# Attention in a two-layer decoder trunk: scores and values as products on halves of the array, denominators ahead of the transposes, two orders changed

## The chip, the cores and the metric

The kernel runs on one core of one Trainium2 chip. The metric is the device time of one execution in microseconds (us); lower is better. The engines are PE (TensorE matmul; PEld is its weight load), DVE (VectorE), ACT (ScalarE), POOL (GpSimd) and SP, which here only issues transfers.

## The reference, cut to what matters

The trunk has 256 positions, a width of 1024 and two layers. Each layer is a feed-forward block (width 2816), a mixer, and another feed-forward block. The mixer of the first layer joins a sliding-window attention with a multi-scale pooling; the mixer of the second is a recurrence (RWKV7). The attention, which the change is about:

```python
q = rms_norm(q, q_norm)          # 8 heads of 64
k = rms_norm(k, k_norm)          # 2 heads of 64, each serves 4 query heads
scores = einsum('bnqhgd,bnkhd->bhgnqk', qb, kb) * 64 ** -0.5
scores = where(valid, scores - slopes * dist, -inf)      # window of 128 positions
m = maximum(max(scores), sink)
p = exp(scores - m)
denom = sum(p) + exp(sink - m)
out = einsum('bhgnqk,bnkhd->bnqhgd', p / denom, vb)
```

The queries of positions 0 to 127 see one block of 128 keys; those of positions 128 to 255 see two blocks, so 256 keys.

## The kernel before, in words

The 256 positions are two halves `h` = 0 and 1 of 128 rows each. Projections and feed-forward products are made of three products on high and low parts of the numbers in fp32r (`mm3`, L225 to L227). The weights are loaded in pieces of 128x1024 (`split`), cast by ACT to the high part (`whi`, L215); DVE or POOL make the low part (`wlo`, L220, L218). The small products of attention, pooling and recurrence are in f32; each of them stands in the trace as two instructions on PE (transposes as one).

**Layer 0's mixer** is cut into steps, and the string `ORDER_AB` (L34) says in which order they are written. `I` projects keys, values, queries and the pooling input of a half (`ab_in`). `N1` normalizes the rows of the second half. `P` is the pooling (`ab_pool`, L440): ACT scales the accumulator into `p` (L442), four band products (L448, in the second half also L450), ACT's copy of the means `mp` (L452), four products with `pool_w` (L455), DVE's scale (L456) and `hilo` (a cast on ACT, L288, and a subtraction on DVE, L289), which writes one half of the columns for the output projection. `K`, `Q`, `S`, `E`, `F` are the five parts of `ab_mix` (L459), each up to a `yield`:

- `K`: the keys are normalized (power and scale on POOL), written twice side by side into `kd`, transposed, and copied by ACT into `kbd` (L481), a block-diagonal tile that was zeroed once (L403): rows 0 to 63 hold the keys for one query head, rows 64 to 127 the same keys for the other.
- `Q`: the queries are normalized in the same way and transposed; `qT` holds two heads in its 128 rows.
- `S`: for each pair of heads one product on all 128 rows gives the scores of both side by side (L506, 2 x 128 columns in the first half, 2 x 256 in the second). DVE adds the distance term for each head (L509) and takes the maximum of each pair (L512).
- `E`: maximum with the sink, then eight exponentials on ACT, one for each head, with the sum in the accumulator (L523); the denominators and their reciprocals `rden` on DVE (L525, L527).
- `F`: PE transposes the exponentials (L536), ACT and DVE copy them to `pT` (L538, L540). With `pT` as the loaded operand (128 columns) and 64 columns of values moving, PE makes `ops` (L545). DVE multiplies by `rden` (L547), PE transposes the result (L550), and `hilo` makes the attention half of the input of the output projection.

`O` is that projection (`ab_out`, with `w_out`), which takes the pooling's columns first (`ABP`); `B` begins the feed-forward block behind it (norm, transposes on PE, eight casts with the gain on ACT, L299). The PSUM banks of a half are taken in turn from two names: `ms` and `gu`, or `tp` and `gu`, where `gu` has two buffers.

**Layer 1's mixer** is written in the order of the string `ORDER` (L32). Two of its steps matter. `k00` is `c_gram` for the first eight heads and the first rows: two grams on 64x64 halves (`heads2`, L733), each followed by a masking on DVE (L816), transposes (`turn2`, L740) and a copy on ACT (L819). `d00` is `c_rest`: products (L893), a masking on DVE (L895) and three rounds of products and an addition on DVE (L904). Both take their banks in turn from the same four, `acc00` to `acc11`. Near them stands `t1` (`c_substitute`), a chain of small DVE instructions (L853, L855) that begins with what a transfer through DRAM brings (`L<-ds`).

The order in which instructions are written is not the order in which they run: the framework's scheduler simulates the engines and gives each engine a fixed list, by priority (the written order) among what its simulation takes to be ready. On the chip each engine goes through its list in order.

Of the kernel before, what the change touches and what calls it, by code (L numbers as in the profile page):

```python
# [8 lines left out]
F32 = mybir.dt.float32  # L9
F32R = mybir.dt.float32r  # L10
BF16 = mybir.dt.bfloat16
AF = mybir.ActivationFunctionType
ALU = mybir.AluOpType
AX = mybir.AxisListType
# [14 lines left out]
QB = (0, 0)  # L29
QV = (0, 0)  # L30
NPT = 2
ORDER = 'L k o0 r p00 R p01 b00 b01 s0 o1 p10 p11 v g V t0 D0 X l0 b11 b10 s1 D1 d00 k00 k01 k11 t1 d01 k10 v10 v01 l1 d10 c00 c10 d11 v00 c01 v11 W0 P00 P01 O00 c11 P10 P11 O10 Y W1 O01 a0 O11 a1'  # L32
BIG = 8
ORDER_AB = 'I0 N1 K0 Q0 S0 P0 E0 I1 K1 Q1 P1 F0 S1 E1 F1 O0 B0 O1 B1'  # L34
ABP = (2, 3, 0, 1)
POOL_AB = 2
ABB = (('ms', 'gu'), ('tp', 'gu'))
# [1 line left out]
HALVES = (slice(0, 64), slice(64, 128))  # L39
# [87 lines left out]
def bc(ap, axis, n):  # L127
    a = ap.unsqueeze(axis)
    shape = list(a.shape)
    shape[axis] = n  # L130
    return a.broadcast_to(shape)


class Trunk:
# [263 lines left out]
    def ab_setup(self):  # L398
        nc, A = self.nc, self.A
        s = self.ab = {}  # L400
        self.mixer_pool("ab")
        s["kbd"] = self.mx.tile([128, 2, 2, 256], F32, name="kbd")
        nc.gpsimd.memset(s["kbd"], 0.0)  # L403
        def load(n, shape, src=None):
            a = self.now.rearrange("p a (b c) -> p a b c", b=2) if len(shape) == 4 else self.now
            return self.const(n, shape, src=src, pool=self.mx, after=a[:, 0] if len(shape) == 2 else a)

        s["qkg"] = load("qk_gain", [128, 2])
        s["sink"] = load("sink", [128, 8], A["sinks"][0].partition_broadcast(128))
        s["ps"] = load("pool_scale", [128, 4])  # L410
        s["edge"] = load("edge", [128, 4, 16])
        s["dist"] = load("dist", [128, 256])
        s["pw"] = load("pool_w", [128, 4, 128])
        s["band"] = load("band", [128, 4, 2, 128])
        s["v"] = [self.mx.tile([128, 2, 64], F32, name=f"v{h}") for h in range(2)]
        s["p"] = [self.mx.tile([128, 512], F32, name=f"p{h}") for h in range(2)]
# [42 lines left out]
    def ab_mix(self, h, st):  # L459

        nc, A, ab = self.nc, self.A, self.ab
        acc, kv, r0, bank = st["acc"], st["kv"], st["r"], st["bank"]
        one, small = self.mx, self.msmall
        v, kbd = ab["v"][h], ab["kbd"]

        tk = small.tile([128, 128], F32, name=f"tk{h}", bufs=1)
        nc.scalar.activation(out=tk, in_=kv[:, :128], func=AF.Square, scale=r0)
# [6 lines left out]
                                in1=bc(bc(rk, 2, 2), 3, 64), op=ALU.mult)  # L474
        nc.scalar.activation(out=v, in_=kv[:, 128:].rearrange("p (a b) -> p a b", a=2), func=AF.Copy, scale=r0)
        kps = bank([128, 2, 128])
        for a in range(2):
            nc.tensor.transpose(kps[:, a, :], kd[:, a].rearrange("p a b -> p (a b)"), self.ident)
        for b in range(2):
            r = slice(64 * b, 64 * b + 64)  # L480
            nc.scalar.activation(out=kbd[r, :, b, 128 * h:128 * h + 128], in_=kps[r], func=AF.Copy,  # L481
                                 scale=ab["qkg"][r, 1:2])
        yield

        tq = one.tile([128, 512], F32, name=f"tq{h}")
# [6 lines left out]
                                in0=acc[0].rearrange("p (a b) -> p a b", a=8), in1=bc(rq, 2, 64), op=ALU.mult)  # L492
# [3 lines left out]
        qT = one.tile([128, 4, 128], F32, name=f"qT{h}")  # L496
# [3 lines left out]
        k0 = 0 if h else 128  # L500
        nk = 256 - k0
        s = one.tile([128, 8, nk], F32, name=f"s{h}")
        mx = small.tile([128, 8], F32, name=f"mx{h}")
        for i in range(4):
            sps = bank([128, 2, nk])
            nc.tensor.matmul(sps, qT[:, i, :], kbd[:, i // 2, :, 0:nk], start=True, stop=True)  # L506
            for j in range(2):

                nc.vector.scalar_tensor_tensor(out=s[:, 2 * i + j, :], in0=ab["dist"][:, k0:],  # L509
                                               scalar=-8.0 * 2.0 ** -(2 * i + j + 1), in1=sps[:, j, :],  # L510
                                               op0=ALU.mult, op1=ALU.add)
            nc.vector.tensor_reduce(out=mx[:, 2 * i:2 * i + 2], in_=s[:, 2 * i:2 * i + 2, :], axis=AX.X, op=ALU.max)  # L512
        yield

        nc.vector.scalar_tensor_tensor(out=mx, in0=mx, scalar=0.125, in1=ab["sink"], op0=ALU.mult, op1=ALU.max)
# [9 lines left out]
        nc.vector.tensor_tensor(out=den, in0=den, in1=es, op=ALU.add)  # L525
        rden = small.tile([128, 8], F32, name=f"rden{h}")
        nc.vector.reciprocal(out=rden, in_=den)  # L527
        yield
        nb = nk // 128
        mh, ml = st["x"]  # L530
        pT = one.tile([128, nb, 8, 128], F32, name=f"pT{h}")
        for b in range(nb):
            for q in range(2):
                tp = bank([128, 4, 128])
# [3 lines left out]
                    nc.scalar.copy(out=pT[:, b, 4 * q:4 * q + 4, :], in_=tp)  # L538
                else:
                    nc.vector.tensor_copy(out=pT[:, b, 4 * q:4 * q + 4, :], in_=tp)  # L540
        ops = bank([128, 8, 64])
        for i in range(8):
            for b in range(nb):
                vv = ab["v"][h - nb + 1 + b]
                nc.tensor.matmul(ops[:, i, :], pT[:, b, i, :], vv[:, i // 4, :], start=b == 0, stop=b == nb - 1)  # L545
        o = one.tile([128, 512], F32, name=f"tq{h}")
        nc.vector.tensor_tensor(out=o.rearrange("p (a b) -> p a b", a=8), in0=ops, in1=bc(rden, 2, 64), op=ALU.mult)  # L547
        tp = bank([128, 4, 128])
        for i in range(4):
            nc.tensor.transpose(tp[:, i, :], o[:, i * 128:(i + 1) * 128], self.ident)  # L550
        self.hilo(tp, mh.tiles[0], ml.tiles[0])
        yield

# [505 lines left out]
def trunk(tc, A, out, stop=None):  # L1059
    with ExitStack() as ctx:  # L1060
# [49 lines left out]
        for h in range(2):  # L1110
# [4 lines left out]
            for n in "KQSEF":  # L1115
                do[f"{n}{h}"] = lambda h=h: next(mix[h])
        for n in ORDER_AB.split():
            do[n]()
        with t.pool("pre") as t.pre:
# [20 lines left out]
            def tail(h):  # L1140
                t.add_acc(h, t.cs["acc", h])
                t.ffn_begin(S[3], h, 3)
# [13 lines left out]
            for G in range(2):  # L1156
# [16 lines left out]
                do[f"a{G}"] = lambda h=G: tail(h)  # L1173
            for n in ORDER.split():
                do[n]()
# [24 lines left out]
```

## Time and profile before

| what | us |
|---|---|
| median of three runs (lowest, highest) | 1110.58 (1107.48, 1113.06) |
| the profiled execution's own time | 1113.11 |
| its span, first to last instruction | 1111.3 |
| PE busy in the span | 1056.5 |
| DVE busy | 640.1 |
| ACT busy | 517.1 |
| POOL busy | 206.5 |

The profile is that of one execution. Busy times are sums over the whole span, while the change touches two short stretches of it: layer 0's mixer, from about 206 to 291 us, and a part of layer 1's mixer, near 800 us. So the rows below are cut by stretch. In the rows of the timeline the first number is the start in us, the second the time from there to the end of the last instruction of the row; several instructions of one kind in a row are merged, with their count as x2, x16. An idle time stands in brackets, with what ended it. Instructions of PE overlap: the time that one costs is the distance of the starts, and not its duration.

### The profile page before, as it was taken

To read this page: it belongs to the slowest core of one execution; us is meant where nothing else is said; L and a number is where in the kernel's file an instruction comes from. 1 tells how busy PE (TensorE), PEld (TensorE's weight loads), DVE (VectorE), ACT (ScalarE), POOL (GpSimd) and SP (SyncE) were. 2 spreads that over 40 slices of the span, in tenths; PEclk is the share of its full clock that TensorE was granted. 3 is DMA by queue.
4 is the path that set the end of the run, shared out by engine and by line. 5 is a ranking of instruction groups with operands and counts; after the bars stand their busy time and mean duration, and the time that the engine had idled before them with its cause. 6 is when DMAs were issued, how large, how long until landed. Compare 5 with 4: busy or idle time off the path is not lost.

```text
span 1111.3 us, 16514 instructions
## 1 busy us (share of the span) xinstructions
PE 1056.5 (95%) x6332; PEld 856.9 (77%) x6332; DVE 640.1 (58%) x966; ACT 517.1 (47%) x876; POOL 206.5 (19%) x199
## 2 busy tenths in 40 slices
PE   7999999999999999999999999998698889999998
PEld 5788887778788888778888877875697667888886
DVE  6655454566564554665555546897574666464642
ACT  7544444574554443554444435675122355454440
POOL 2101110340300101010101101174201530101100
PEclk9999999999999999999999999999899798999999
DMA  8764664453465555556565544652422246555631
GB/s 288 245 208 160 228 193 139 149 175 101 141 220 188 194 164 191 170 156 196 165 222 158 183 121 127 181 161 53 110 61 67 69 144 218 207 186 174 204 99 38
DMA packets 70671, 179.33 MB, mean 161 GB/s; under 512 B 23872, under 2 KB 24512, under 8 KB 70592
## 3 DMA queue, kind: packets, MB, share of 16 engines
q1 hardware_dynamic: 70304, 178.19, 50.5%
q8 instruction: 50, 0.82, 0.3%
q14 instruction: 29, 0.24, 0.1%
q10 hardware_dynamic: 288, 0.09, 0.0%
HBM read 174.58 MB, written 3.67 MB: 160 GB/s over the span
## 4 chain that ended last, share of the span: by engine, by line
PE 81%; DVE 6%; DMA 4%; ACT 4%; issue 3%; POOL 1%; SPq 0%; DVEq 0%; ACTq 0%; POOLq 0%
PE gu L225 14%; PE gu L227 14%; PE gu L226 14%; PE acc L225 10%; PE acc L227 10%; PE acc L226 10%; DMA raw<-w_gu 2%; DVE wlo L220 2%; PE acc L733 2%; PE tp L351 2%; ACT whi L215 1%; PE gu L733 1%; DMA hn<-w_rkvo 1%; PE tp L733 1%; PE ms L733 0%
## 5 line engine op out<-in xcount | busy, mean ns | idle before, releaser
L220 DVE TENSOR_TENSOR wlo<-raw,whi 128x1024 fp32r<-128x1024 f32 x261 | 341.0, 1308 | 182.5 <-ACT whi L215 179.2
L215 ACT CAST whi<-raw 128x1024 fp32r<-128x1024 f32 x306 | 320.6, 1049 | 198.1 <-PE gu L227 72.8
L225 PE MATMUL gu<-whi,xh 128*128 128x512 f32 x704 | 286.7, 408 | 2.5 <-ACT xh L299 2.2
L227 PE MATMUL gu<-whi,xl 128*128 128x512 f32 x704 | 279.2, 398 | 2.0 <-DVE xl L300 1.8
L226 PE MATMUL gu<-wlo,xh 128*128 128x512 f32 x704 | 279.4, 397 | 0.1
L218 POOL TENSOR_TENSOR wlo<-raw,whi 128x1024 fp32r<-128x1024 f32 x45 | 108.3, 2407 | 616.3 <-ACT whi L215 610.8
L227 PEld LDWEIGHTS gu<-whi,xl 128*128 128x128 f32 x704 | 133.4, 189 | 35.6 <-DVE xl L300 4.8
L225 PEld LDWEIGHTS gu<-whi,xh 128*128 128x128 f32 x704 | 133.4, 190 | 33.1 <-ACT xh L299 6.2
L226 PEld LDWEIGHTS gu<-wlo,xh 128*128 128x128 f32 x704 | 133.7, 190 | 27.5 <-DVE wlo L220 0.6
L225 PE MATMUL acc<-whi,ah 128*128 128x512 f32 x352 | 139.0, 395 | 4.0 <-ACT ah L288 4.0
L226 PE MATMUL acc<-wlo,ah 128*128 128x512 f32 x352 | 137.5, 391 | 0.0
L227 PE MATMUL acc<-whi,al 128*128 128x512 f32 x352 | 131.1, 394 | 0.1
L342 ACT ACTIVATE t<-gu,rh 128x256 f32<-128x256 f32 x88 | 41.4, 473 | 119.9 <-PE gu L227 119.9
L343 DVE SCALAR_TENSOR_TENSOR t<-t,gu 128x256 f32<-128x256 f32 x88 | 36.6, 418 | 87.3 <-ACT t L342 87.2
L289 DVE TENSOR_TENSOR al<-tp,ah 128x256 fp32r<-128x256 f32 x88 | 37.1, 421 | 84.5 <-ACT ah L288 84.4
L288 ACT CAST ah<-tp 128x256 fp32r<-128x256 f32 x88 | 32.4, 369 | 111.0 <-PE tp L351 110.9
L225 PEld LDWEIGHTS acc<-whi,ah 128*128 128x128 f32 x352 | 66.0, 188 | 20.4 <-ACT ah L288 5.7
L227 PEld LDWEIGHTS acc<-whi,al 128*128 128x128 f32 x352 | 65.8, 188 | 15.6 <-DVE al L289 0.5
L226 PEld LDWEIGHTS acc<-wlo,ah 128*128 128x128 f32 x352 | 66.1, 188 | 15.0
L226 PE MATMUL acc<-wlo,xh 128*128 128x512 f32 x160 | 64.5, 403 | 0.0
L227 PE MATMUL acc<-whi,xl 128*128 128x512 f32 x160 | 63.9, 405 | 0.6 <-DVE xl L289 0.6
L225 PE MATMUL acc<-whi,xh 128*128 128x512 f32 x160 | 62.4, 408 | 0.7 <-ACT xh L288 0.7
(495 smaller groups left out, 1117.6 us busy)
## 6 DMA issues: line engine op xcount, KB each, us to landing
raw<-w_gu SPq DMA_DIRECT2D x176, 512.0 KB, 4.3
raw<-w_dn SPq DMA_DIRECT2D x88, 512.0 KB, 4.2
raw<-w_rkvo SPq DMA_DIRECT2D x24, 512.0 KB, 3.6
raw<-w_qp SPq DMA_DIRECT2D x8, 512.0 KB, 4.3
raw<-w_out SPq DMA_DIRECT2D x8, 512.0 KB, 3.5
hn<-w_rkvo SPq DMA_DIRECT2D x16, 256.0 KB, 2.8
ch<-chan SPq DMA_DIRECT2D x10, 256.0 KB, 5.1
x<-x SPq DMA_DIRECT2D x4, 256.0 KB, 5.2
```

The lines of the kernel that those rows point to most:

```text
L215: nc.scalar.copy(out=hi, in_=raw)
L218: nc.gpsimd.tensor_tensor(out=lo, in0=raw, in1=hi.bitcast(F32), op=ALU.subtract)
L220: nc.vector.tensor_tensor(out=lo, in0=raw, in1=hi.bitcast(F32), op=ALU.subtract)
L225: mm(out, xh, wh, start=start, stop=False)
L226: mm(out, xh, wl, start=False, stop=False)
L227: mm(out, xl, wh, start=False, stop=stop)
L288: self.nc.scalar.copy(out=hi, in_=src)
L289: self.nc.vector.tensor_tensor(out=lo, in0=src, in1=hi.bitcast(F32), op=ALU.subtract)
L342: nc.scalar.activation(out=t, in_=gu[:, :256], func=AF.Tanh, scale=rh)
L343: nc.vector.scalar_tensor_tensor(out=t, in0=t, scalar=1.0, in1=gu[:, :256], op0=ALU.add, op1=ALU.mult)
L351: nc.tensor.transpose(ps[:, j, :], t[:, j * 128:(j + 1) * 128], self.ident)
L733: self.nc.tensor.matmul(out[rs], a[rs], b[rs], start=start, stop=stop)
```

## The change

- `kbd` and its memset go. `kT` (128 x 2 x 256) holds the transposed keys without zeros: rows 0 to 63 and rows 64 to 127 hold the same keys, and one ACT copy for each half of the positions writes it in place of two.
- Scores: for each group `a` of four heads two banks are taken, one for each half of the rows. Each product takes 64 rows of `qT` and of `kT` and gives the scores of one head; the two halves of the rows write to different banks. One maximum for four heads takes the place of one for two.
- Denominators: at the end of `E`, eight ACT instructions for each half of the positions scale the exponentials by `rden`, ahead of the transposes of `F`.
- Values: 64 columns of values are now the loaded operand and 128 columns of `pT` move. The two heads of a pair write to the two halves of the PSUM partitions, so the result comes out transposed; the multiplication by `rden` and the transposes of the output (L547, L550) go.
- Order: in `ORDER_AB` `P0` moves from behind `S0` to ahead of `Q0`, and `P1` from behind `Q1` to behind `E1`. In `ORDER` `k00` and `d00` change places.

```diff
-ORDER = '... s1 D1 d00 k00 k01 k11 t1 ...'
+ORDER = '... s1 D1 k00 d00 k01 k11 t1 ...'
-ORDER_AB = 'I0 N1 K0 Q0 S0 P0 E0 I1 K1 Q1 P1 F0 S1 E1 F1 O0 B0 O1 B1'
+ORDER_AB = 'I0 N1 K0 P0 Q0 S0 E0 I1 K1 Q1 F0 S1 E1 P1 F1 O0 B0 O1 B1'
...
-        s["kbd"] = self.mx.tile([128, 2, 2, 256], F32, name="kbd")
-        nc.gpsimd.memset(s["kbd"], 0.0)
+        s["kT"] = self.mx.tile([128, 2, 256], F32, name="kT")
...
-        for b in range(2):
-            r = slice(64 * b, 64 * b + 64)
-            nc.scalar.activation(out=kbd[r, :, b, 128 * h:128 * h + 128], in_=kps[r], func=AF.Copy,
-                                 scale=ab["qkg"][r, 1:2])
+        nc.scalar.activation(out=kT[:, :, 128 * h:128 * h + 128], in_=kps, func=AF.Copy, scale=ab["qkg"][:, 1:2])
...
-        for i in range(4):
-            sps = bank([128, 2, nk])
-            nc.tensor.matmul(sps, qT[:, i, :], kbd[:, i // 2, :, 0:nk], start=True, stop=True)
-            for j in range(2):
-                nc.vector.scalar_tensor_tensor(out=s[:, 2 * i + j, :], in0=ab["dist"][:, k0:],
-                                               scalar=-8.0 * 2.0 ** -(2 * i + j + 1), in1=sps[:, j, :],
-                                               op0=ALU.mult, op1=ALU.add)
-            nc.vector.tensor_reduce(out=mx[:, 2 * i:2 * i + 2], in_=s[:, 2 * i:2 * i + 2, :], axis=AX.X, op=ALU.max)
+        for a in range(2):
+            sps = [bank([128, 2, nk]) for b in range(2)]
+            for i in range(2):
+                for b, rs in enumerate(HALVES):
+                    nc.tensor.matmul(sps[b][:, i, :], qT[rs, 2 * a + i, :], kT[rs, a, 0:nk], start=True, stop=True)
+            for n in range(4):
+                j = 4 * a + n
+                nc.vector.scalar_tensor_tensor(out=s[:, j, :], in0=ab["dist"][:, k0:], scalar=-8.0 * 2.0 ** -(j + 1),
+                                               in1=sps[n % 2][:, n // 2, :], op0=ALU.mult, op1=ALU.add)
+            e = slice(4 * a, 4 * a + 4)
+            nc.vector.tensor_reduce(out=mx[:, e], in_=s[:, e, :], axis=AX.X, op=ALU.max)
...
+        for i in range(8):
+            nc.scalar.activation(out=s[:, i, :], in_=s[:, i, :], func=AF.Copy, scale=rden[:, i:i + 1])
         yield
...
-        ops = bank([128, 8, 64])
-        for i in range(8):
-            for b in range(nb):
-                vv = ab["v"][h - nb + 1 + b]
-                nc.tensor.matmul(ops[:, i, :], pT[:, b, i, :], vv[:, i // 4, :], start=b == 0, stop=b == nb - 1)
-        o = one.tile([128, 512], F32, name=f"tq{h}")
-        nc.vector.tensor_tensor(out=o.rearrange("p (a b) -> p a b", a=8), in0=ops, in1=bc(rden, 2, 64), op=ALU.mult)
         tp = bank([128, 4, 128])
         for i in range(4):
-            nc.tensor.transpose(tp[:, i, :], o[:, i * 128:(i + 1) * 128], self.ident)
+            for b in range(nb):
+                for j, rs in enumerate(HALVES):
+                    nc.tensor.matmul(tp[rs, i, :], ab["v"][h - nb + 1 + b][:, i // 2, :], pT[:, b, 2 * i + j, :],
+                                     start=b == 0, stop=b == nb - 1)
         self.hilo(tp, mh.tiles[0], ml.tiles[0])
```

## Rows read from the trace of the kernel before

**Rows 1.** The page, part 1: busy time, share of the span, instructions.

```profile
PE 1056.5 (95%) x6332; PEld 856.9 (77%) x6332; DVE 640.1 (58%) x966; ACT 517.1 (47%) x876; POOL 206.5 (19%) x199
```

**Rows 2.** Busy time by stretch (us, engines, granted clock, DMA share, GB/s).

```profile
206.00:291.00 85.00, 81.15 (x436) 66.70 (x435) 49.14 (x91) 47.15 (x107) 26.95 (x39) 1.00 0.40 125
...
796.00:805.00 9.00, 0.66 (x12) 0.42 (x10) 2.73 (x14) 0.00 (x0) 0.00 (x0) 0.80 0.57 126
291.00:745.00 454.00, 447.79 (x2034) 362.17 (x2033) 269.21 (x373) 222.33 (x349) 74.85 (x58) 1.00 0.55 176
```

**Rows 3.** Waits of PE from 206 to 291: total us, times, longest.

```profile
PE ms L455 <- ACT mp L452: 1.7, 1, 1.7
...
PE acc L227 <- DVE xl L289: 0.6, 1, 0.6
```

**Rows 4.** The chain that ended last, 200 to 300 us: start, us, what.

```profile
219.69 0.47 ACT kbd L481
...
221.88 0.43 PE ms L506 x2
...
255.10 0.86 PE tp L506 x2
...
256.89 0.44 PE ms L550 x4
```

**Rows 5.** Timeline of PE near 252 us: value products, then scores.

```profile
251.81 1.45 PE L545 MATMUL gu<-v,pT 128*128 128x64 f32 x12
253.10 1.08 PE L506 MATMUL gu<-kbd,qT 128*128 128x512 f32 x2
```

**Rows 6.** Timeline of PE from 745 us: full products, then 64x64 halves.

```profile
744.95 0.40 PE L227 MATMUL acc<-whi,xl 128*128 128x512 f32 x1
745.27 1.09 PE L733 MATMUL tp<-a,b 64*64 64x128 f32 x16
746.20 0.63 PE L740 MATMUL gu<-ident,b 64*64 64x64 f32 x16
746.66 1.04 PE L733 MATMUL gu<-a,b 64*64 64x128 f32 x16
747.54 0.63 PE L740 MATMUL ms<-ident,b 64*64 64x64 f32 x16
```

**Rows 7.** Timeline at 205 us: matmuls on the full array and a load.

```profile
205.17 0.39 PE L225 MATMUL acc<-whi,ah 128*128 128x512 f32 x1
205.17 0.19 PEld L226 LDWEIGHTS acc<-wlo,ah 128*128 128x128 f32 x1
...
205.40 0.40 PE L226 MATMUL acc<-wlo,ah 128*128 128x512 f32 x1
```

**Rows 8.** Timeline of ACT, 266 to 274 us: exponentials and gain casts.

```profile
266.64 0.49 ACT L523 ACTIVATE s<-s,nm 128x256 f32<-128x256 f32 x1
267.05 0.19 ACT L523 ACTIVATION_READ_ACCUMULATOR s<-s,nm 128x1 f32 x1
...
271.65 0.35 ACT L299 ACTIVATE xh<-acc,gain 128x128 fp32r<-128x128 f32 x1
...
273.30 0.62 ACT L299 ACTIVATE xh<-acc,gain 128x128 fp32r<-128x128 f32 x2
```

**Rows 9.** Timeline, 270 to 282 us: denominators, ACT's next idle time.

```profile
270.22 0.17 DVE L525 TENSOR_TENSOR den<-den,es 128x8 f32<-128x8 f32 x1 [1.16 <-ACT s L523]
...
281.57 0.47 ACT L342 ACTIVATE t<-gu,rh 128x256 f32<-128x256 f32 x1 [5.85 <-PE gu L227]
```

**Rows 10.** Timeline of layer 1's mixer, 801 to 811 us.

```profile
801.89 0.16 DVE L853 TENSOR_TENSOR pr<-L,XL 128x2 f32<-128x2 f32 x1 [7.49 <-DMA L<-ds]
...
804.76 2.26 PE L733 MATMUL acc<-tmp 64*64 64x64 f32 x32 [8.34 <-DVE tmp L904]
...
806.80 1.71 PE L733 MATMUL acc<-a,k 64*64 64x128 f32 x16
...
810.21 1.09 PE L733 MATMUL acc<-a,k 64*64 64x128 f32 x16 [1.23 <-DVE b L904]
```

More of the change, by code (lines that the diff above doesn't have):

```diff
@@ L31 @@
 NPT = 2
-ORDER = 'L k o0 r p00 R p01 b00 b01 s0 o1 p10 p11 v g V t0 D0 X l0 b11 b10 s1 D1 d00 k00 k01 k11 t1 d01 k10 v10 v01 l1 d10 c00 c10 d11 v00 c01 v11 W0 P00 P01 O00 c11 P10 P11 O10 Y W1 O01 a0 O11 a1'
+ORDER = 'L k o0 r p00 R p01 b00 b01 s0 o1 p10 p11 v g V t0 D0 X l0 b11 b10 s1 D1 k00 d00 k01 k11 t1 d01 k10 v10 v01 l1 d10 c00 c10 d11 v00 c01 v11 W0 P00 P01 O00 c11 P10 P11 O10 Y W1 O01 a0 O11 a1'
 BIG = 8
-ORDER_AB = 'I0 N1 K0 Q0 S0 P0 E0 I1 K1 Q1 P1 F0 S1 E1 F1 O0 B0 O1 B1'
+ORDER_AB = 'I0 N1 K0 P0 Q0 S0 E0 I1 K1 Q1 F0 S1 E1 P1 F1 O0 B0 O1 B1'
 ABP = (2, 3, 0, 1)
@@ L463, in ab_mix @@
         one, small = self.mx, self.msmall
-        v, kbd = ab["v"][h], ab["kbd"]
+        v, kT = ab["v"][h], ab["kT"]
         tk = small.tile([128, 128], F32, name=f"tk{h}", bufs=1)
```

## The prediction

> **What bounds the kernel now.** I read the page's first part, then the busy time by stretch, then who waited for whom on PE. PE is busy for 95% of the span [rows 1]. Nearly everything edited lies in the attention stretch from 206 to 291 us: there PE is busy for 81.15 of 85 us, at the full granted clock, while ACT has 47.15 us of work and DVE 49.14 [rows 2]. PE's waits there are few; the ones that count below are 1.7 and 0.6 us long [rows 3]. So this stretch is a stream of matmuls with short holes, and what is taken off PE's queue should show, as long as other matmuls are ready. The feed-forward stretch behind it (291 to 745 us) has PE busy for 447.79 of 454 us [rows 2], so time won earlier is carried through it. The swap of `k00` and `d00` lies in a different place: a hole of 9 us in layer 1 in which PE has 0.66 us of work and the clock's mean falls to 0.80 [rows 2].
>
> **Scores (L506).** Each f32 product is issued as two instructions. Two of them take 0.43 us with 256 columns (first half of the rows, four products) and 0.86 us with 512 (second half, four) [rows 4]: 1.72 + 3.44 = 5.16 us. The new form has twice as many products, each on 64 rows and with half the columns. If the two row halves of the array run side by side, the time is that of half the columns: 2.58 us, a gain of 2.58. No row shows 64 rows by 128 columns; the nearest is the gram of layer 1 on 64x64 halves, where 16 instructions of 128 columns take 0.88 us, 0.055 each [rows 6], half of the 0.107 that such an instruction needs alone by the scores' row (0.43/2 for 256 columns). The bounds are 0 and 2.58; I take 2.58, since the row shows halves side by side.
>
> **Values and probabilities (L545, L547, L550).** 48 instructions of 64 columns stand there; twelve take 1.29 us (251.81 to 253.10), 0.107 each [rows 5], so they cost 5.14 us and are set by the load of 128 columns rather than by the 64 that move. Eight transposes of the output at 0.44 us for four [rows 4] add 0.88. The new form also has 48 instructions, now of 128 moving columns on 64 loaded ones: 0.107 each if one after the other (nothing gained but the transposes), 0.055 side by side [rows 6], 2.57 us in all. Gain 0.88 to 3.45; I take 3.45 for the same reason. A multiplication on DVE per half goes too, at no gain: DVE is far from full.
> Here a row and a rule meet. The load for L226 starts at 205.17 us together with L225's matmul on all 128 rows, which is in flight until 205.56 [rows 7]. The Trainium skill, "TensorE: Matmul & The Clock Gate", Part 3, says that a weight load overlaps a matmul in flight only when it goes to another row group. By that rule the column halves, which all use every row, would load between matmuls: the values' gain would stay at its lower bound and the whole would come out at 1106.8 us. Rows 7, where the load runs under a matmul on the same rows, speak against it.
>
> **Changes of shape.** From a full-array matmul to one on halves takes 0.32 us (744.95 to 745.27) against 0.23 between two full ones (205.17 to 205.40): 0.09 [rows 6, 7]. I take the same on the way back. The scheduler mixes these groups with the output projection; two blocks for each of scores and values in each half make 8 blocks, 8 x 0.18 = 1.4 us of loss (bounds 0.7 with four blocks, 4.3 with every one of the 24 pairs alone).
>
> **Denominators on ACT.** Sixteen scalings are added. With 128 columns one gain cast of the next norm lasts 0.35 us and two last 0.62, so each follows the one before by 0.27; with 256 columns an exponential gives way to its accumulator's read after 0.41 us (266.64 to 267.05) [rows 8]. That is 8 x 0.27 + 8 x 0.41 = 5.4 us. Of the four copies into `kbd`, at 0.47 us, two go: -0.94 [rows 4]. Net +4.5 us on ACT. What covers them: ACT's work in the stretch is 47 of 85 us, and after its work of the second half it stood idle for 5.85 us [rows 2, 9]. But now the transposes of the probabilities wait for the denominators (270.22 us in the second half) and the scalings, where before they followed the exponentials, and behind the scalings in ACT's queue stand the gain casts of the next norm, which the first gate products need [rows 8, 9]. With no cover the cost is 5.4 us; with full cover 0. The scheduler can put projections and pooling there; I charge 1.5 us, about half of the second half's 3.3; the first half's scalings lie where the projection of the second half's rows keeps PE going.
>
> **Order of the stretch.** `P0` now comes ahead of `Q0`, `S0` and `E0`: three ACT passes of 512 columns (some 0.7 us each, an estimate from the 0.27 and 0.41 above), two DVE passes and 16 PE instructions of 128 columns (1.7 us at 0.107). It issues no DMA, nothing on SP and nothing on POOL; what it is moved past (`Q0`'s power and scale on POOL, its transposes, `E0`'s exponentials) it can hold up by those 2.1 us of ACT at most, and the projection `I1` keeps PE going then. Today it runs so late that PE waits 1.7 us for the copy of its means, and 0.6 us more for its low half before the output projection [rows 3]. Early pooling removes both: -2.3 us (bounds 0 and -2.3). `P1` goes behind `E1` and `F0` ahead of `S1`: the work of `P1` becomes filling for the second half's softmax, counted in the 1.5 above. The memset of `kbd` on POOL goes at no gain: no wait in the stretch is for it [rows 3].
>
> **`k00` ahead of `d00`.** DVE waits 7.49 us for the transfer of `L` at the head of `t1`; the update of `d00` behind it in DVE's queue holds PE for 8.34 us, and `k00`, which takes the same four banks later, can only run at 806.80 and 810.21 [rows 10]. Put first, it can run ahead of the hole: a gram with its transposes takes 1.34 us at full clock (746.20 to 747.54), its two 2.7 [rows 6]. Against it: `d00` starts later, so that more of its rounds fall behind the same DVE wait. One round costs PE 2.04 us at the lower clock (804.76 to 806.80). No DMA is issued by either. Bounds -2.7 and +2.0; I take -1.0: one of the two grams won, less a handover, since 806.80 shows half of `k00` standing between the hole and the next step.
>
> **Sum.** -2.58 - 3.45 + 1.4 + 1.5 - 2.3 - 1.0 = -6.4 us. The profiled execution took 1113.11 us, 1.8 of it around its span of 1111.3; so it would take 1106.7. It stands 2.5 above the median of the runs, so in terms of the median 1110.58 the forecast is 1104.2 us.
>
> **Rivals.**
> 1. *The halves don't overlap.* Then only the output's transposes are saved: -0.88 + 1.4 + 1.5 - 2.3 - 1.0 = -1.3, 1109.3 us. The 64x64 rows speak against it, but no row has 64 by 128 or 128 by 64, so 0.10. If it holds for the values alone, the loss is 2.57: 1106.8 us. The rule named above would lead to that half of it.
> 2. *ACT becomes the bound* (slower). In the softmax of each half PE finds nothing ready while ACT scales; then PE's savings only lengthen its waits, and the net ACT time counts: +4.5 - 1.0 = +3.5, 1114.1 us, and to 1116 and more if the casts of the next norm are late as well. It decides when the ready work in PE's queue is shorter than the 3.3 us of the second half's scalings. For it: the norm casts stand behind them. Against: ACT's 5.85 us of idleness right after, and the output projection as filling [rows 9]. 0.10.
> 3. *`d00` falls wholly behind the transfer.* Two more rounds at 2.04 us and a handover of 0.3 each (my guess), some 4.7 us, less the 2.7 of `k00`: +2.0 where I took -1.0, so 1107.2 us. 0.14.
> 4. *The time is given back.* The weights of the next feed-forward arrive at their own pace, so that the savings of the stretch turn into waits for casts: only the -1.0 is left, 1109.6 us. Against it: PE at 447.79 of 454 us and no long wait in the stretch for a cast of weights [rows 2, 3]. 0.06.
>
> **How the numbers follow.** My forecast has 0.60. Its own range is 1100 to 1108: from -2.7 in layer 1 and four blocks of shape changes to no gain in layer 1 and a charge of 3 on ACT. Half a per cent is 5.55 us, about what a measurement of this kernel can tell from no change; it is reached at 1105.0. About seven tenths of my forecast and some of rivals 3 and 1 lie beyond: faster 0.50. The rest of it and most of rivals 1, 3 and 4, with part of 2, make same 0.40; slower 0.10 is rival 2 with a bad layer 1. The range runs from 1099 to 1112, taking in rivals 1, 3 and 4 and leaving out rival 2 and the best ends.
>
> **What will show it.** Right: scores of 64 rows in pairs at about 0.11 (128 columns) and 0.21 us (256); the value products at about 0.055 each; no L550; no wait of PE for the copy of `P0`'s means; PE's stretch from 206 to its first steady gate product shorter by 5 us; `k00` before the 8 us hole. Wrong: pairs at double these times (rival 1), new waits of PE on the scalings or on the norm's casts of 3 us and more (rival 2), a longer hole and later `d01` in layer 1 (rival 3), PE waits on casts of weights after 291 us (rival 4).

## The result, and the profile after

The changed kernel takes 1125.66 us (median of 6 runs, 1121.4 to 1128.99) where the kernel before took 1112.07 beside it (6 runs): a ratio of 1.0123, 95% interval 1.0092 to 1.0153. It is slower, by 13.6 us; the forecast was 1104.2, and the range ended at 1112. The profiled execution took 1124.33 us, its span is 1122.5 us (before: 1113.11 and 1111.3).

The page's first part, busy time of each engine over the span [rows 1]:

```profile
PE 1065.6 (95%) x6340; PEld 861.9 (77%) x6340; DVE 640.1 (57%) x960; ACT 522.9 (47%) x890; POOL 208.3 (19%) x198
```

PE is 9 us busier than before, though its matmuls were to become cheaper. ACT has 5.8 us more where the prediction's net was 4.5: the sixteen scalings took 2.45 + 3.31 = 5.76, and the saving of two copies doesn't show in the sum.

To place the loss, I cut the program at the additions into the residual on DVE, which every version has. The attention of layer 0 lies between the last L372 ahead of it and the last L378 behind it. Timeline of DVE, kernel before:

```profile
207.80 0.69 DVE L372 SCALAR_TENSOR_TENSOR x<-acc,x 128x512 f32<-128x512 f32 x1
...
289.56 0.68 DVE L378 TENSOR_TENSOR x<-acc,x 128x512 f32<-128x512 f32 x1
```

And the same of the changed kernel:

```profile
207.52 0.69 DVE L372 SCALAR_TENSOR_TENSOR x<-acc,x 128x512 f32<-128x512 f32 x1
...
301.12 0.68 DVE L378 TENSOR_TENSOR x<-acc,x 128x512 f32<-128x512 f32 x1
```

The attention went from 289.56 - 207.80 = 81.8 us to 93.6: 11.8 us longer, against 11.2 us between the two profiled executions. The two feed-forward stages behind it take the same as before within 0.1 us, the mixer of layer 1 takes 1.0 us more (239.4 against 238.3) and the rest 1.6 less (0.3 ahead of the attention, 1.3 behind the mixer). So the time was lost in the attention, and nothing behind it gave it back. This cut is steady: two programs with the same attention, the kernel before and one that differs from it only in layer 1, gave 81.8 and 82.1; the changed kernel and such a sister of it 93.6 and 94.3.

Busy time by stretch of the changed kernel, columns as in [rows 2]:

```profile
206.00:291.00 85.00, 77.87 (x389) 60.35 (x388) 41.50 (x78) 46.43 (x111) 22.10 (x27) 0.88 0.28 91
253.00:273.25 20.25, 17.51 (x62) 12.45 (x62) 7.14 (x17) 11.70 (x46) 0.00 (x0) 0.50 0.00 1
260.00:270.00 10.00, 10.00 (x37) 7.28 (x36) 4.95 (x10) 2.63 (x10) 0.00 (x0) 0.50 0.01 2
```

Before, this stretch ran at a granted clock of 1.00 throughout. Now there are 20 us at 0.50, that is 1.2 of 2.4 GHz: PE is busy for 17.51 us there. At the full clock that would be work of about half the time (products of 512 columns start 0.43 us apart there, 0.23 at 1.00), so by estimate up to 8.8 us are lost to the clock; less, where other engines would have made PE wait. Waits of PE from 206 to 302 us [rows 3]:

```profile
PE gu L538 <- ACT s L529: 2.7, 1, 2.7
PE acc L227 <- DVE xl L289: 1.6, 1, 1.6
PE tp L491 <- DVE tq L487: 1.4, 1, 1.4
PE tp L505 <- DVE s L509: 0.9, 1, 0.9
PE tp L225 <- ACT xh L299: 0.3, 1, 0.3
PE gu L454 <- ACT mp L451: 0.2, 1, 0.2
```

Of the two waits that early pooling was to remove, the one for the copy of P0's means went from 1.7 to 0.2 us, as forecast; the one for its low half (L227 for L289) grew from 0.6 to 1.6. A new one stands at the head: the transposes of the probabilities (L538) wait 2.7 us for the scalings (L529). Where it comes from is seen in the timeline of all engines, cut to the steps that follow on one another:

```profile
217.52 0.69 DVE L487 TENSOR_TENSOR tq<-acc,rq 128x512 f32<-128x512 f32 x1 [2.50 <-POOL rq L486]
...
230.27 0.69 ACT L441 ACTIVATE p<-acc,rs 128x512 f32<-128x512 f32 x1 [2.26 <-PE acc L227]
...
235.75 0.72 PE L447 MATMUL ms<-band,p 128*128 128x128 f32 x5
...
237.15 1.16 PE L454 MATMUL gu<-mp,pool_w 128*128 128x128 f32 x8 [0.21 <-ACT mp L451]
238.14 0.60 PE L491 MATMUL ms<-ident,tq 128*128 128x128 f32 x4
...
240.71 0.37 PE L505 MATMUL gu<-kT,qT 64*128 64x128 f32 x1
240.72 0.37 PE L505 MATMUL ms<-kT,qT 64*128 64x128 f32 x1
...
252.51 1.59 PE L505 MATMUL tp<-kT,qT 64*128 64x256 f32 x4 [0.92 <-DVE s L509]
...
256.39 2.45 ACT L529 ACTIVATE s<-s,rden 128x128 f32<-128x128 f32 x8 [0.53 <-DVE rden L527]
...
256.84 1.35 PE L538 MATMUL gu<-ident,s 128*128 128x128 f32 x4 [2.74 <-ACT s L529]
```

The queries of the first half (`tq`) are ready at 218.2 us, but their transposes (L491) run at 238.14. Before, they ran at 218.97, by the timeline of PE:

```profile
218.97 0.60 PE L495 MATMUL ms<-ident,tq 128*128 128x128 f32 x4
```

Between the two stands P0. K0, P0 and Q0 of a half take their PSUM banks from one turn (`ABB`, `ms` and `gu` for the first half), in the order of the program. With P0 ahead of Q0, P0's band products hold `ms`, and Q0's transposes have to wait until they were made and copied out. P0 in turn needs the second column of the input projection, which ends at 230. So the part that could have started waits for the part that couldn't, and scores, exponentials and scalings of the first half come some 20 us later, next to those of the second half.

Where they ran in pairs, the products did what was forecast: for the first four heads of the first half, the two row halves start 0.01 us apart (240.71, 240.72); the other scores ran one row half after the other. Value products follow one another at 0.067 us (twelve in the 0.81 us from 281.29 to 282.10, the step back to full matmuls included):

```profile
281.29 0.88 PE L548 MATMUL gu<-pT,v 128*64 128x128 f32 x12
282.10 0.50 PE L225 MATMUL gu<-whi,xh 128*128 128x512 f32 x1
```

In layer 1 the grams and transposes of `k00` did run ahead of the hole, as forecast, but the hole stayed, with one round of `d00` behind it as before. Timeline of the changed kernel, the lines that answer to [rows 10]:

```profile
811.42 1.92 SPq L837 DMA_DIRECT2D L<-ds  x4
...
814.86 0.16 DVE L852 TENSOR_TENSOR pr<-L,XL 128x2 f32<-128x2 f32 x1 [8.17 <-DMA L<-ds]
...
817.17 1.12 PE L732 MATMUL acc<-tmp 64*64 64x64 f32 x16 [8.58 <-DVE tmp L903]
```

### The profile page after: what moved, and what is told of

It is laid out like the page before. It is cut to its first block, busy times and chain, and to the rows that moved or that the text cites. A ratio compares the mean times of both kernels' runs of the same rounds, so it can differ in the third digit from the quotient of the medians.

```text
span 1122.5 us, 16523 instructions
## 1 busy us (share of the span) xinstructions
PE 1065.6 (95%) x6340; PEld 861.9 (77%) x6340; DVE 640.1 (57%) x960; ACT 522.9 (47%) x890; POOL 208.3 (19%) x198
## 4 chain that ended last, share of the span: by engine, by line
PE 80%; DVE 6%; DMA 5%; ACT 4%; issue 3%; POOL 1%; SPq 1%; DVEq 0%; ACTq 0%; POOLq 0%
PE gu L225 14%; PE gu L227 14%; PE gu L226 14%; PE acc L225 10%; PE acc L227 10%; PE acc L226 10%; DVE wlo L220 2%; DMA raw<-w_gu 2%; PE tp L351 2%; ACT whi L215 1%; DMA hn<-w_rkvo 1%; PE gu L732 1%; PE acc L732 1%; PE tp L732 1%; PE ms L732 0%
## 5 line engine op out<-in xcount | busy, mean ns | idle before, releaser
L227 PE MATMUL gu<-whi,xl 128*128 128x512 f32 x704 | 278.5, 397 | 0.6 <-DVE xl L300 0.5
L227 PEld LDWEIGHTS gu<-whi,xl 128*128 128x128 f32 x704 | 133.2, 189 | 32.6 <-DVE xl L300 1.8
L227 PE MATMUL acc<-whi,al 128*128 128x512 f32 x352 | 131.0, 394 | 0.1
L289 DVE TENSOR_TENSOR al<-tp,ah 128x256 fp32r<-128x256 f32 x88 | 37.0, 421 | 82.8 <-ACT ah L288 82.8
L227 PEld LDWEIGHTS acc<-whi,al 128*128 128x128 f32 x352 | 65.8, 188 | 15.6 <-DVE al L289 0.5
L227 PE MATMUL acc<-whi,xl 128*128 128x512 f32 x160 | 63.9, 404 | 1.6 <-DVE xl L289 1.6
```

Of the source, the lines that this page charges most:

```text
L227: mm(out, xl, wh, start=False, stop=stop)
L289: self.nc.vector.tensor_tensor(out=lo, in0=src, in1=hi.bitcast(F32), op=ALU.subtract)
```

## The experiments

All of them in one table: median time, ratio to the kernel before run beside it with its interval, the length of the attention (last L372 to last L378, from the profile) and of layer 1's mixer (from the third of the four L372 that end the second feed-forward behind the attention, to the last L378). The two lengths are those of one profiled execution each.

| kernel | us | ratio | attention | layer 1 |
|---|---|---|---|---|
| before | 1112.07 | 1 | 81.8 | 238.3 |
| changed | 1125.66 | 1.0123 [1.0092, 1.0153] | 93.6 | 239.4 |
| e1 | 1122.37 | 1.0096 [1.0069, 1.0123] | 89.8 | 240.3 |
| e2 | 1116.01 | 1.0045 [1.003, 1.006] | 86.1 | 238.6 |
| e3 | 1107.56 | 0.9962 [0.995, 0.9974] | 76.6 | 238.5 |
| e4 | 1120.43 | 1.0081 [1.0062, 1.01] | 94.3 | 234.1 |
| e5 | 1105.98 | 0.9954 [0.9937, 0.9971] | 76.6 | 237.5 |
| e6 | 1112.09 | 0.9999 [0.9983, 1.0015] | 80.2 | 239.4 |
| e7 | 1116.51 | 1.0069 [1.0044, 1.0094] | 80.5 | 241.9 |
| e8 | 1112.77 | 1.0014 [1.0001, 1.0027] | 82.1 | 239.1 |
| e9 | 1114.99 | 1.0035 [1.0021, 1.0049] | 81.5 | 242.5 |
| e10 | 1106.26 | 0.995 [0.9931, 0.9969] | 77.1 | 238.4 |
| e11 | 1110.86 | 0.9993 [0.9978, 1.0007] | 79.2 | 239.0 |
| e12 | 1105.11 | 0.9947 [0.9926, 0.9967] | 76.6 | 237.7 |
| e13 | 1122.51 | 1.0102 [1.0076, 1.0128] | 90.7 | 239.5 |
| e14 | 1116.52 | 1.0053 [1.0037, 1.007] | 88.5 | 236.6 |

The kernel before had medians of 1110.7 to 1112.1 in the several comparisons.

**e1: the changed kernel with the attention's parts in the order of before.**

```
-ORDER_AB = 'I0 N1 K0 P0 Q0 S0 E0 I1 K1 Q1 F0 S1 E1 P1 F1 O0 B0 O1 B1'
+ORDER_AB = 'I0 N1 K0 Q0 S0 P0 E0 I1 K1 Q1 P1 F0 S1 E1 F1 O0 B0 O1 B1'
```

> The changed kernel with the old ORDER_AB alone. Bank theory (P0 written ahead of Q0 takes the bank ms first, Q0's transposes wait for it until 238 us, and the first half's softmax falls behind the projections): Q0's transposes back at about 218 us, the exponentials of the first half near 226 us, no stretch at half clock, 1104 to 1109 us, a little faster than before. ACT theory (the sixteen scalings, 5.8 us in the profile, set the pace): 1118 us or more, since they stay. Shape theory (products on halves let the clock fall): the half clock stays near 260 us, 1118 us or more.

Measured: 1122.37 us, attention 89.8. Q0's transposes are back at 219.07 us, as the bank theory had it, but its time is missed. The turn of the banks is therefore not the whole story: with P0 back, 8.0 us of loss against the kernel before remain in the attention. Waits of PE from 206 to 302 us:

```profile
PE gu L538 <- ACT s L529: 4.8, 1, 4.8
PE ms L454 <- ACT mp L451: 2.7, 1, 2.7
PE gu L225 <- ACT xh L299: 1.2, 1, 1.2
```

The scalings now hold PE for 4.8 us in the second half. What stands in ACT's queue there, by the timeline:

```profile
274.71 1.98 ACT L215 CAST whi<-raw 128x1024 fp32r<-128x1024 f32 x2
276.59 3.31 ACT L529 ACTIVATE s<-s,rden 128x256 f32<-128x256 f32 x8
279.79 0.60 ACT L299 ACTIVATE xh<-acc,gain 128x128 fp32r<-128x128 f32 x2
```

Casts of weights ahead of the scalings, the scalings, and the next norm's casts behind them: this is the mechanism of rival 2, with P1 no longer there to fill the time. The clock is at 0.50 twice here, for 3.4 us from 241.3 and for 6.8 us from 275.4; each time it falls during one of the first two waits.

**e2: the kernel before with the new order of the parts.** The reverse of that edit, on the kernel before.

> The kernel before with the new ORDER_AB alone: no products on halves, no scalings. Bank theory: Q0's transposes at about 238 us, the half clock appears here too, 1124 to 1132 us (more than the changed kernel, since the products are longer). ACT theory and shape theory: 1109 to 1114 us, as before.

Measured: 1116.01 us, attention 86.1, in the range of no theory. Q0's transposes run at 238.93 us, as the bank theory had it; the half clock that it expected didn't come: from 200 to 300 us the clock stays at 1.00. The order alone costs 4.3 us of attention there.

**e3: the changed kernel, the pool's products in banks of their own.** In `ab_pool` alone `bank` becomes a turn over the two banks of the half's accumulator, which are free once the projections were read (cut out of a longer assignment).

```
-bank = st["bank"]
+bank = self.banks((f"acc{h}0", f"acc{h}1"))
```

> The changed kernel, its order kept, but the pooling takes its two banks from the accumulators that it has just read (acc01, acc00 in the first half, acc11, acc10 in the second) and no longer from the turn of ms and gu. Bank theory: Q0's transposes at about 218 us although P0 stands ahead of Q0, no half clock, 1102 to 1108 us. Priority theory (P0 comes first in the scheduler's list whatever the banks): Q0's transposes stay near 238 us, 1122 us or more. ACT theory: 1118 us or more.

Measured: 1107.56 us, faster than both, attention 76.6 us: 17 us come off the changed kernel by the choice of a bank for two small steps. Q0's transposes run before P0's products again, though P0 is still written ahead of them, and the clock is 1.00 from 200 to 330 us:

```profile
218.39 0.60 PE L491 MATMUL ms<-ident,tq 128*128 128x128 f32 x4
```

**e4: the changed kernel with `d00` ahead of `k00`, as before the change.**

> The changed kernel with d00 ahead of k00 again, all else as changed. If layer 1 is neutral, as the two profiles have it (the part behind 291 us differs by less than 0.5 us between them once the start is lined up): 1122 to 1129 us, the changed kernel's time. If the swap had won 1 us as predicted: 1 us more. If the swap were the loss: 1112 to 1116 us.

Measured: 1120.43 us, between the theories: 5.2 us faster than the changed kernel by the medians, though the intervals of the ratios overlap a little; by the profiles, layer 1 is 5.3 us shorter (234.1 against 239.4).

**e5: e3 with `d00` ahead of `k00`.**

> The changed kernel with the pool's products in the accumulator's banks, as in e3_pool_own_banks (1107.56 us), and with d00 ahead of k00 in layer 1, as before the change. Theory (moving k00 ahead of d00 costs time by itself): the layer-1 mixer, from the third x += acc of L372 to the last of L378, was 238.5 in e3, 239.4 in the changed kernel and 234.1 with the old order, so 2 to 5 us come off e3: 1102.5 to 1105.5, and the wait of the W products for ACT stands some 2 us earlier in the layer. Rival (what the swap costs hangs on how late the layer starts, since the kernel before, with the old order, took 238.3 as e3 did): 1107 to 1108, layer 1 at 238 to 239.

Measured: 1105.98 us, 1.6 below e3 (the intervals overlap), between the two theories: layer 1 took 237.5. The waits of PE from 206 to 302 us are 2.7 us in all, none of them for the scalings; the first stands behind the attention, which ends at 285.8:

```profile
PE tp L351 <- DVE t L344: 1.5, 1, 1.5
PE tp L491 <- DVE tq L487: 0.7, 1, 0.7
PE gu L548 <- DVE pT L542: 0.5, 1, 0.5
```

**e6: the kernel before with the new order and the pool's own banks.** The edits of e2 and e3 together, products and denominators untouched.

> The kernel before with the new order of the attention's parts (P0 ahead of Q0, P1 after E1) and the pool's products in the accumulator's banks; scores, values and denominators as they were. Theory A (the banks and the place of P1 are what e3 gained, the products on halves little): the attention, from the last L372 ahead of it to the last L378, takes 76 to 79 us (e3: 76.6, before: 81.8), time 1104.5 to 1108.5. Rival B (the products on halves are what e3 gained): 80 to 82 us, time 1109.5 to 1112.

Measured: 1112.09 us, no change, attention 80.2: rival B by the attention, and a tenth over its range by the time. The banks give 5.9 us against e2 (86.1), and what e5 has over this kernel, 3.6 us of attention and 6.1 of the medians, is due to the products on halves, with the scalings that go with them.

**e7: the changed kernel with P0 alone put back.**

```
-ORDER_AB = 'I0 N1 K0 P0 Q0 S0 E0 ...
+ORDER_AB = 'I0 N1 K0 Q0 S0 P0 E0 ...
```

> The changed kernel with P0 alone put back behind S0; P1 stays behind E1. Theory A (P0's turn in the banks is what delays the queries; the scalings cost nothing while the second pool lies beside them): Q0's transposes near 219 us, no stretch at half clock, attention 77 to 83 us, time 1107 to 1114. Rival B (the eight scalings on ACT bound the second half wherever P0 stands): the wait of the probability transposes for the scaled rows stays at 2.5 to 5 us and the time at 1118 to 1122.

Measured: 1116.51 us, attention 80.5: theory A by the attention, 2.5 us over its range by the time, and its "no stretch at half clock" was a miss: the mean is 0.66 from 240 to 250 us, around the first wait below. The transposes run at 218.65 us and no wait of PE for the scalings is left:

```profile
PE ms L454 <- ACT mp L451: 2.6, 1, 2.6
PE gu L225 <- ACT xh L299: 1.7, 1, 1.7
```

So P0's place is worth 93.6 - 80.5 = 13.1 us of attention (9.2 of the medians), and P1 behind E1 is worth 89.8 - 80.5 = 9.3 (5.9 of the medians) by e1: it is the cover for the scalings. (Both kernels have a short stretch at half clock, 6.8 us here and 10.2 in e1.) Part of what e7 wins is lost again behind the attention: the next feed-forward's first products wait 1.7 us for the norm's casts and that stage is 3.0 us longer (192.7 against 189.7), and its layer 1, with the swap, took 241.9.

**e8: the kernel before with `k00` ahead of `d00` and nothing else.**

> The kernel before with k00 ahead of d00 in layer 1 and nothing else. The prediction's term: -1.0 us, so 1110.0 to 1111. Theory (the swap costs time by itself): the W products wait 2 to 5 us later in the layer, time 1113 to 1116.5. Rival (the swap costs only in a kernel whose layer starts late): within 1 us of the kernel before.

Measured: 1112.77 us, ratio 1.0014 [1.0001, 1.0027], a loss of 0.1 to 3.0 us between the two theories; the prediction's gain of 1.0 is excluded.

**e9: e1 without the scalings.** The kernel leaves out the division by the denominators, as do e10 and e13.

```
-        for i in range(8):
-            nc.scalar.activation(out=s[:, i, :], in_=s[:, i, :], func=AF.Copy, scale=rden[:, i:i + 1])
```

> e1_old_mixer_order (the changed kernel with the attention's parts in the order of before, 1122.37 us, attention 89.8 us) without the sixteen scalings on ACT: the division by the denominators is left out of the computation. Theory A (with P1 ahead of E1 nothing lies beside the scalings, and they hold the second half): the 4.8 us wait of the probability transposes goes, and with it the stretch below full clock behind it; attention 78 to 82 us, time 1109 to 1114. Rival B (the stretch comes from the pool's wait for mp, 2.7 us, and the scalings fill idle time of ACT): attention 86 us or more, time 1118 to 1122.

Measured: 1114.99 us, attention 81.5 where e1 had 89.8: theory A by the attention, 1.0 over its range by the time. Without cover, 5.76 us of ACT's work cost 8.3 us of attention and 7.4 of the medians. That is more than their length, and part of it is the clock: it is at 1.00 throughout the attention here, where e1 had 10.2 us at 0.50. Of PE's waits in the attention, the one for the scalings is gone:

```profile
PE ms L454 <- ACT mp L451: 1.5, 1, 1.5
PE acc L227 <- DVE xl L289: 0.8, 1, 0.8
```

**e10: e5 without the scalings.** The same lines removed from e5.

> e5_own_banks_old_layer1 (1105.98 us, attention 76.6 us) without the sixteen scalings on ACT: the division by the denominators is left out of the computation. Theory A (beside P1 and the next norm the scalings are covered): within 1 us of e5, attention 75.5 to 77. Rival B (the prediction's charge of 1.5 us, or ACT's net 4.5 us, is on the path even there): attention 72 to 75.2 us, time 1101.5 to 1104.5.

Measured: 1106.26 us, attention 77.1, against 1105.98 and 76.6 with them. Where P1 and the output projection lie beside them, the same sixteen instructions cost nothing that can be measured.

**e11: e5 with values and denominators as before the change.** Sixteen value products a block, the multiply by `rden` on DVE and the four transposes are back; the scalings go.

> e5_own_banks_old_layer1 (1105.98 us) with the values and the denominators as before the change (sixteen products 128x64 a block, one multiply by the reciprocals on DVE, four transposes), so that of the products only the scores are on halves. e6, with neither, took 80.2 us for the attention. Prediction's terms: the values' 3.45 us less the charge of 1.5 for the scalings, so 2 us lost against e5: attention 78 to 79, time 1107 to 1109. Rival (the scores hold the whole gain of halves, the values' gain is eaten by the scalings): attention 76 to 77, time 1105 to 1107.

Measured: 1110.86 us, attention 79.2. The values on halves, scalings included, are worth 2.6 us of attention and 4.9 of the medians. The scores on halves are worth 80.2 - 79.2 = 1.0 by e6, 1.2 by the medians, whose intervals overlap.

**e12: e5 with P0 put back.**

> e5_own_banks_old_layer1 (1105.98 us, attention 76.6 us) with P0 put back behind S0. The prediction's term for P0 ahead of Q0 was -2.3 us: with banks of its own, and no turn to wait for, it should now show, attention 78.5 to 79.5, time 1107.5 to 1109. Rival (with own banks the place of P0 costs and gains nothing): attention 76 to 77.5, time 1105 to 1107.

Measured: 1105.11 us, attention 76.6, as in e5. With banks of its own P0's place costs and gains nothing, so the 2.3 us that were forecast for it aren't there either. By the traces P0's band products run at about the same time in both orders, 237.8 us in e3 and 238.4 here: writing them ahead brings them no earlier. Beside e7, which has P0 in the same place in shared banks, the attention is 3.9 us shorter, so banks of its own are worth something beyond the turn. This, e5 and e3 are the complete versions that beat both kernels.

**e13: the changed kernel without the scalings.**

> The changed kernel (1125.66 us, attention 93.6 us) without the sixteen scalings on ACT: the division by the denominators is left out of the computation. Theory A (the late queries leave TensorE with nothing beside the first half's exponentials and scalings, 2.7 us of waiting, and the half clock follows from that hole): without the scalings the hole is short, no stretch at half clock, attention 84 to 88 us, time 1116 to 1120. Rival B (the late queries alone bring the half clock): attention 90 us or more, time 1122 to 1125.

Measured: 1122.51 us, attention 90.7, and the clock is down as before (from 252.8 to 269.8 us); rival B. The scalings cost 2.9 us of attention in the changed kernel, and 3.2 by the medians, whose intervals overlap. Busy time by stretch of this kernel:

```profile
250.00:260.00 10.00, 8.53 (x31) 5.10 (x30) 4.73 (x15) 3.81 (x18) 0.00 (x0) 0.64 0.01 5
260.00:270.00 10.00, 10.00 (x37) 8.03 (x37) 3.75 (x8) 4.30 (x17) 0.00 (x0) 0.51 0.00 0
```

So the scalings are not needed for the half clock: the late queries suffice, with the products on halves. In the changed kernel too the clock falls (253.0) before PE's wait for them begins (254.1).

**e14: the kernel before with P0 alone ahead of Q0, in shared banks.**

```
-ORDER_AB = 'I0 N1 K0 Q0 S0 P0 E0 ...
+ORDER_AB = 'I0 N1 K0 P0 Q0 S0 E0 ...
```

> The kernel before with P0 alone moved ahead of Q0, in the banks that it shares with K0 and Q0; P1 stays where it was. Theory A (the bank turn by itself delays Q0's transposes from 219 to about 238 us, and the first half's scores with them): attention 85 to 90 us, time 1114 to 1120. Rival B (without the scalings the late queries are made up for, and e2's 4.3 us come from P1 behind E1): attention 81 to 83 us, time 1110 to 1113.

Measured: 1116.52 us, attention 88.5; theory A. One part moved in the kernel before, nothing else, and the transposes move from 218.97 us to this, by the timeline of PE:

```profile
241.34 0.60 PE L495 MATMUL ms<-ident,tq 128*128 128x128 f32 x4
```

That is 6.7 us of attention. The clock stays at 1.00 from 230 us on; ahead of that, and ahead of the late transposes, it is at 0.50 for 3.4 us from 223.9 on (0.83 in the mean of 220 to 230), by estimate up to 1.7 us of the 6.7. The changed kernel pays 13.1 for the same move; it has the 20 us at the lower clock (by estimate up to 8.8 us), so I put the difference of 6.4 down to that, which no run shows by itself.

## Why the prediction was wrong

**The step that failed: "Order of the stretch", -2.3 us with bounds 0 and -2.3.** It asked what P0 could hold up and answered by its ACT passes: "it can hold up by those 2.1 us of ACT at most". It went through the queues and left out the resource that P0, K0 and Q0 share, the banks. The turn makes Q0 wait not only for P0's work but first for P0's input, the last column of a projection (230 us in the changed kernel, where Q0's transposes then run at 238.14). e14 shows this alone (+6.7 us of attention; 1116.52 against 1110.72 beside it, +5.8), e7 shows it in the changed kernel (+13.1), and e12 shows the term itself to be 0 when the banks are apart. With the banks apart and everything else as changed (e3), the time is 1107.56 us, inside the range of the forecast. No bound on the bad side stood in the sum, because no wait in the kernel before showed the turn: there P0 always came after Q0. The lines that could have shown it were the order of allocation in `ab_pool` and `ab_mix` together with the time at which acc[1] ends.

**The charge for the scalings, +1.5, was right by its condition only.** Their size was: 2.45 + 3.31 = 5.76 us against 5.4. With P1 and the output projection beside them they cost nothing (e10), without them 8.3 us (e9 against e1). In the changed kernel they are late with the queries and hold PE for 2.7 us (2.9 of attention by e13). Rival 2, at 0.10, had the mechanism, and e1 shows it at more than its price (8.3 us of attention against 4.5 on ACT, the clock included); but the order that the change brings with it moves P1 to where it covers the second half, and the wait of 2.7 us stands in the first.

**The values, -3.45, were right.** PE's busy time for them goes from 6.18 us (L545) and 1.20 (L550) before to 3.95 (L548) in e5, -3.43. From start to start, as the prediction prices them, and with the changes of shape in them, it is about 6.3 to 3.6 us, -2.7, which is the term less half of the +1.4 charged for those changes; the changes of shape have no run of their own. The Trainium skill, "TensorE: Matmul & The Clock Gate", Part 3, has a weight load overlap a matmul in flight only when it goes to another row group. These products all use every row, and at 0.067 us each, where one after the other was priced at 0.107, they speak against that. Rival 1 falls for them.

**The scores, -2.58, came to about half.** PE's busy time by source line from 206 to 302 us is 6.34 us for L506 before, 4.98 for L505 in e5, -1.36; e11 against e6 has 1.0 in the attention, not clear of noise in the medians. Timeline of PE in e5, first half:

```profile
222.33 0.27 PE L505 MATMUL gu<-kT,qT 64*128 64x128 f32 x1
222.34 0.27 PE L505 MATMUL ms<-kT,qT 64*128 64x128 f32 x1
222.44 0.27 PE L505 MATMUL gu<-kT,qT 64*128 64x128 f32 x1
222.45 0.27 PE L505 MATMUL ms<-kT,qT 64*128 64x128 f32 x1
...
222.66 0.61 PE L505 MATMUL gu<-kT,qT 64*128 64x128 f32 x4
...
224.06 0.71 PE L505 MATMUL ms<-kT,qT 64*128 64x128 f32 x4
```

Pairs 0.11 us apart, as forecast, for the first four heads; the other four run one half after the other, because, by the code, `ms` has one buffer, which DVE must have read first, while `gu` has two. In the second half `tp` takes the place of `ms`, and the last four heads fare alike (249.17 to 257.20 us).

**`k00` ahead of `d00`, -1.0, had the wrong sign.** It costs 0.1 to 3.0 us alone (e8), 1.6 in e3 against e5 and 5.2 in the changed kernel against e4; of these only e8 is clear of noise, and just so. Rival 3 supposed that `d00` falls behind the transfer; one round of it did, as before. What the traces show is that the transfer is late: the reads of `L` start 131.4 us after the third L372 in the median of the seven profiles with the swap (130.9 to 133.4), and 129.3 in the nine without it (128.7 to 131.7, so the two overlap). Queue of SP in e3, then in e5 (issue of the reads, the third L372 at 662.98 and 664.98):

```profile
794.09 2.69 SPq L837 DMA_DIRECT2D L<-ds  x4
```

```profile
793.81 2.01 SPq L837 DMA_DIRECT2D L<-ds  x4
```

That is 131.1 and 128.8 us after the mark. The delay is there long before the reads. DVE's reduction `ssk`, which waits for ACT, starts 105.1 to 106.6 us after the mark in the seven profiles with the swap and 103.0 to 104.1 in the nine without; the first write of `ds`, which the reads of `L` bring back, starts at 125.6 to 126.6 and 123.0 to 124.1. Timeline of DVE in the kernel before, then in e8 (the marks are 668.59 and 668.21):

```profile
771.99 0.69 DVE L785 TENSOR_REDUCE ssk<-tmp 128x8 f32<-128x512 f32 x1 [0.98 <-ACT tmp L783]
```

```profile
773.35 0.69 DVE L785 TENSOR_REDUCE ssk<-tmp 128x8 f32<-128x512 f32 x1 [2.91 <-ACT tmp L783]
```

In e8 the transposes of `k00` begin 94.9 us after the mark; they stand in PE's list among the products ahead of `ssk`. If they are the cause, the prediction counted what `k00` fills and not what it is put in front of. Which of its instructions hold up which step wasn't tried.

**Carried through.** That time won or lost in the attention passes through the feed-forward stages held (rival 4 falls): 189.6 and 189.3 us after the change, 189.7 and 189.3 before, 189.9 and 189.3 in e3. The exceptions are in the first of the two stages: e7, with its late casts (192.7), and e1 and e13 (190.7 both).

By its own terms without the two reorderings, the sum was -2.58 - 3.45 + 1.4 + 1.5 = -3.1 us; e5 against e6 has -3.6 in the attention. That they agree is in part luck: the scores gave about 1.2 less than their term, and the scalings cost 1.5 less.

What stays open: why the clock fell for so long in the changed kernel, in e4 and in e13 and not in e2, which has the same order and the same late queries. In the changed kernel PE was busy for 0.59 and 0.49 of the two microseconds ahead of the fall at 253, in e2 for 0.97 and 0.49 of the same two; no run separates the smaller products from the hole that they leave.

## What to carry to other kernels

Before a step is moved, ask what it takes its buffers from: if steps share banks in turn, a step that is moved ahead also puts its own input in front of everything behind it in that turn, and this shows in no wait of the profile of before. Give a step whose input comes late banks outside the turn. Added work on an engine that is half idle cost nothing here (e10) or more than its own length (e9 against e1), depending on whether independent matmuls were queued beside it, so the filling has to be moved along with it.

## What was not expected of the hardware

- The granted clock fell to 0.50 at 253 us and stayed there for 20 us although PE was busy for 10.00 of 10.00 us in the middle of it (260 to 270); with whole products in the same order (e2) it stayed at 1.00. By estimate the lower clock cost up to 8.8 us; all waits of PE in the attention together are 7.1.
- The Trainium skill, "Perfetto Trace Analysis", section "Matmuls", recommends that independent groups rotate through different banks, so that copies overlap with the next products. The runs here bound that: a rotation over two banks tied a ready group to one that wasn't, and taking one of the three steps out of it was worth 17.0 us of attention (e3 against the changed kernel).
- The same sixteen scalings cost 8.3 us in e1 (against e9) and nothing in e5 (against e10), with the same length on ACT; in e1 10.2 us at the lower clock are part of it.
